# Reordering an S5 layer's parameter work beside the q, k and v projections of the layer before it

## The chip, the cores and the metric

One core of one Trainium2 chip runs the whole program. The time is device microseconds of one execution; lower is better.

## What is computed

A trunk of two layers over 512 tokens of width 1024, all in fp32. Layer 0 is block-sparse attention with rotary positions beside a multi-scale pooling branch; layer 1 is an S5 state-space branch beside a convolution. The parts that matter here, cut from the reference:

```python
def rope_partial(x):                       # the first 32 of 128 columns of a head
    x1 = xf[..., : ROT_DIM // 2]
    x2 = xf[..., ROT_DIM // 2: ROT_DIM]
    out = jnp.concatenate([x1 * cos - x2 * sin, x2 * cos + x1 * sin, xf[..., ROT_DIM:]], axis=-1)

def even_mixer(h, w_in, pool_w, pool_scale, w_out):
    z = h @ w_in
    q, k, v, ga, pu, gb = jnp.split(z, [A, 2 * A, 3 * A, 4 * A, 4 * A + POOL_WIDTH], axis=-1)
    q = rope_partial(q.reshape(b, s, ATT_HEADS, HEAD_DIM))
    k = rope_partial(k.reshape(b, s, ATT_HEADS, HEAD_DIM))

def s5_ssm(u, lam_re, lam_im, log_dt, b_re, b_im, c_re, c_im, d):
    dt = jnp.exp(log_dt.astype(f32))[:, None]
    mag = jnp.exp(lr * dt)
    ab_re = mag * jnp.cos(li * dt)
    ab_im = mag * jnp.sin(li * dt)
    den = lr * lr + li * li
    num_re = ab_re - 1.0
    f_re = (num_re * lr + ab_im * li) / den
    f_im = (ab_im * lr - num_re * li) / den
    bb_re = f_re[..., None] * br - f_im[..., None] * bi
    bb_im = f_re[..., None] * bi + f_im[..., None] * br
```

The S5 part that comes before any token is seen, `dt` to `bb`, depends on parameters alone. The kernel works it out while layer 0's projections run.

## The kernel before

**Projections.** Every fp32 product is three matmuls on split operands (`mm3`, L104 to L106: high by high, high by low, low by high), 128x512 each. The columns of the input projection are taken in groups: q, k, v (512 columns each), then `pg0`, `pg1`, `ga`. A group has four weight blocks of 512 KB (`raw`, three buffers); ACT rounds each to its high part (`whi`, L169), the DVE makes the low part (`wlo`, L61, two operations of 128x512 a block). `wblock` and `prefetch` run these ahead; SP issues all loads. The output of a group for four tiles of 128 tokens fills four PSUM banks `z`, and there are only four: the next group's tile t starts when this group's tile t has been read out.

**Reading out q and k.** `rope_evac` reads a bank: ACT copies the 96 columns that are not rotated (L602), the DVE rotates the other 32 in four operations:

```python
tt(V, q[:, :, 0:32], zv[:, :, 0:32], cosb, MUL)
tt(V, r[:, :, 0:16], zv[:, :, 16:32], sinb[:, :, 0:16], MUL)
tt(V, r[:, :, 16:32], zv[:, :, 0:16], sinb[:, :, 16:32], MUL)
tt(V, q[:, :, 0:32], q[:, :, 0:32], r, ADD)
```

The first three read the bank, the fourth reads SBUF only. In the trace they are `wt<-z,cs`, `r<-z,cs` (twice) and `wt<-wt,r`. TensorE transposes the rotated tiles (`tp`), and ACT (L109) and DVE (`qk<-tp,qk`) split them.

**S5 parameters.** `s5_loads` loads lambda (`lamn`), `ldt`, the state-major `b` (`b1`, `b2`, rows of 64 bytes), `cn` and `dm`. `s5_small` turns lambda with TensorE (L449, to `lam`) and `cn` (L456), masks `dm` on POOL, and works out exponential, sine and cosine in some hundred DVE operations of 128x32 (`mag`, `sn`, `cnn`, `fr`, `fi`, the powers `AR`, `AI`); then `b1` and `b2` are multiplied: `e<-b,fi`, `b<-b,fr` and their difference on the DVE, `pin<-b,fi`, `b<-b,fr` and their sum on POOL. `b<-b,fr` on the DVE writes over what POOL's `pin` reads. `s5_set_e(c)`, for four sets c, makes `e1` from `AR`, `AI`, `b1`, `b2` in three DVE operations of 128x512, and `g1` in three on POOL, and stores `g1`; `s5_set_p(c)` multiplies `e1` by a matrix `IC` on TensorE (four matmuls of 160 columns, L574) and stores the result. The last `set_p` adds `dm` to `kk` and stores lag kernels with eight DMAs (`kd`, L586). `s5_phasors` makes nine phasors `U` by repeated squaring on POOL, from `sn` and `cnn`: thirteen small operations a round, seven in the first. POOL then fills phasor tables `tab`, the first of which waits for the release of the pool of buffers that all this uses.

**What sets the order.** The list `after[group, block]` says behind which weight block a piece is emitted; `tc.issue_after(instruction)` keeps what is emitted in it behind that instruction. Within these a scheduler orders every engine's instructions by its own simulation; each engine then runs its own order strictly, each instruction waiting for its operands.

## Time and profile before

| | |
|---|---|
| median of 3 runs | 469.53 us (469.25 to 469.56) |
| profiled execution | 469.62 us, span of the trace 467.8 us |
| TensorE (PE) | busy 441.3 us, 94% of the span |
| VectorE (DVE) | 353.4 us, 76% |
| ScalarE (ACT) | 242.9 us, 52% |
| GpSimd (POOL) | 264.4 us, 57% |
| mean granted TensorE clock | 0.991 of full speed |

The profiled execution's own time and the span differ by 1.8 us that lie around the span. q's matmuls run up to 36 us, k's from 38 to 62, v's from 68 to 99.5. A timeline row gives the start, the duration, the engine, the line, the operation with output <- inputs, and in brackets how long the engine stood idle before and which instruction released it. Buffer numbers are left out of names. POOL's spans are rough.

### The profile page before, as it was taken

What the parts mean: (1) busy time and instruction counts of PE and PEld (TensorE: products, weight loads), DVE (VectorE), ACT (ScalarE), POOL (GpSimd) and SP (SyncE); (2) the same over time, 40 slices, a digit from 0 to 9 for tenths busy, and PEclk for the clock granted to TensorE, in tenths of its full rate; (3) what the DMA queues carried; (4) which work ended last, traced back from release to release, by engine and by line L of the source; (5) the groups of instructions that cost most, each with busy time, mean ns of one, the idle gap of its engine ahead of it and who ended that gap; (6) DMA issues with size and microseconds to landing.
All of it is one profiled execution on the core that took longest, in us unless ns stands there. A gap on an engine that the chain in (4) does not pass through costs nothing.

```text
span 467.8 us, 6759 instructions
## 1 busy us (share of the span) xinstructions
PE 441.3 (94%) x2185; PEld 361.9 (77%) x2185; DVE 353.4 (76%) x691; ACT 242.9 (52%) x437; POOL 264.4 (57%) x447
## 2 busy tenths in 40 slices
PE   6998959999988999979999999999999999999994
PEld 5886848888866888858879988777878777778884
DVE  2849999587698696773886397997999898666444
ACT  6644422555734744623685435657966336373421
POOL 1010798999999915480092385676999944421000
PEclk9999989999999999989999999999999999999999
DMA  7874233432422347441044794786434542132013
GB/s 266 191 179 143 91 113 135 120 89 76 135 73 83 118 135 252 158 138 41 3 122 132 179 246 137 208 214 176 125 93 121 153 141 75 71 91 89 1 61 120
DMA packets 62435, 59.58 MB, mean 127 GB/s; under 512 B 20569, under 2 KB 43745, under 8 KB 62400
## 3 DMA queue, kind: packets, MB, share of 16 engines
q1 hardware_dynamic: 62400, 59.16, 42.6%
q8 instruction: 17, 0.28, 0.2%
q14 instruction: 18, 0.15, 0.1%
HBM read 50.62 MB, written 8.52 MB: 126 GB/s over the span
## 4 chain that ended last, share of the span: by engine, by line
PE 59%; DVE 15%; POOL 13%; DMA 4%; ACT 4%; issue 3%; SPq 1%; DVEq 0%; ACTq 0%; POOLq 0%
PE z L104 17%; PE z L105 17%; PE z L106 17%; POOL tab L58 6%; DMA raw<-e_w_in 4%; POOL U L58 3%; DVE wlo L61 3%; POOL pa L58 2%; DVE wt L58 2%; PE s L979 2%; PE y L1014 1%; DVE wt L61 1%; PE y L1011 1%; DVE xh L61 1%; ACT junk L297 1%
## 5 line engine op out<-in xcount | busy, mean ns | idle before, releaser
L58 POOL TENSOR_TENSOR wlo<-raw,whi 128x1024 fp32r<-128x1024 f32 (+2 forms) x50 | 88.4, 1789 | 72.8 <-ACT whi L109 72.4
L104 PE MATMUL z<-hh,whi 128*128 128x512 f32 (+1 forms) x288 | 105.6, 374 | 2.0 <-DVE u L58 2.0
L105 PE MATMUL z<-hl,whi 128*128 128x512 f32 (+1 forms) x288 | 106.3, 370 | 0.0
L106 PE MATMUL z<-hh,wlo 128*128 128x512 f32 (+1 forms) x288 | 105.7, 369 | 0.0
L61 DVE SCALAR_TENSOR_TENSOR acc<-gp,dw,acc 128x512 f32<-128x512 f32 x100 | 75.1, 751 | 2.2
L109 ACT ACTIVATE whi<-raw 128x1024 fp32r<-128x1024 f32 (+2 forms) x54 | 45.3, 873 | 35.6 <-PE z L105 17.7
L104 PEld LDWEIGHTS z<-hh,whi 128*128 128x128 f32 x288 | 54.0, 189 | 12.0 <-DVE u L58 2.4
L106 PEld LDWEIGHTS z<-hh,wlo 128*128 128x128 f32 x288 | 54.4, 189 | 8.6 <-issue 0.2
L105 PEld LDWEIGHTS z<-hl,whi 128*128 128x128 f32 x288 | 54.4, 189 | 8.4 <-issue 0.3
L104 PE MATMUL z<-whi,hh 128*128 128x512 f32 x96 | 39.5, 415 | 9.6 <-DVE r L58 5.5
L61 DVE SCALAR_TENSOR_TENSOR wlo<-raw,gcol,whi 128x512 fp32r<-128x512 f32 x48 | 39.2, 839 | 9.6 <-ACT whi L169 9.5
L169 ACT ACTIVATE whi<-raw,gcol 128x512 fp32r<-128x512 f32 x48 | 32.1, 715 | 22.1 <-PE z L106 10.0
L105 PE MATMUL z<-wlo,hh 128*128 128x512 f32 x96 | 39.3, 412 | 0.0
L106 PE MATMUL z<-whi,hl 128*128 128x512 f32 x96 | 38.8, 404 | 0.0
L58 POOL TENSOR_TENSOR tab<-tab,U 128x4 f32<-128x4 f32 (+6 forms) x112 | 36.6, 358 | 0.0
L104 PEld LDWEIGHTS z<-whi,hh 128*128 128x128 f32 x96 | 18.7, 196 | 14.1 <-issue 5.9
L297 ACT ACTIVATE junk<-z 128x512 bf16<-128x512 f32 (+1 forms) x17 | 9.7, 570 | 30.7 <-PE z L106 30.7
L58 POOL TENSOR_TENSOR tab<-tab 128x4 f32<-128x4 f32 (+6 forms) x56 | 21.8, 409 | 0.0
L105 PEld LDWEIGHTS z<-wlo,hh 128*128 128x128 f32 x96 | 18.9, 196 | 3.6
L106 PEld LDWEIGHTS z<-whi,hl 128*128 128x128 f32 x96 | 18.6, 194 | 3.5
L58 POOL TENSOR_TENSOR pacc<-pacc,lt 128x512 f32<-128x512 f32 x14 | 18.9, 1351 | 0.2
L58 DVE TENSOR_TENSOR hl<-tp,hh 128x512 fp32r<-128x512 f32 x16 | 10.7, 682 | 9.5 <-ACT hh L109 9.5
(325 smaller groups left out, 1015.3 us busy)
## 6 DMA issues: line engine op xcount, KB each, us to landing
raw<-e_w_in SPq DMA_DIRECT2D x15, 512.0 KB, 4.7
raw<-e_w_in SPq DMA_DIRECT2D x18, 256.0 KB, 2.9
raw<-e_w_out SPq DMA_DIRECT2D x8, 512.0 KB, 3.8
raw<-o_w_in SPq DMA_DIRECT2D x16, 256.0 KB, 2.8
rot<-td SPq DMA_DIRECT2D x16, 256.0 KB, 6.0
raw<-o_w_in SPq DMA_DIRECT2D x8, 512.0 KB, 4.3
raw<-o_w_out SPq DMA_DIRECT2D x8, 512.0 KB, 3.7
qk<-x SPq DMA_DIRECT2D x8, 256.0 KB, 5.6
```

The costliest lines, as they stand in the source:

```text
L58: return e.tensor_tensor(o, a, b, op=op)
L61: e.scalar_tensor_tensor(o, a, s, b, op0=op0, op1=op1)
L104: nc.tensor.matmul(p, sh, mh, start=start, stop=False)
L105: nc.tensor.matmul(p, sh, ml, start=False, stop=False)
L106: return nc.tensor.matmul(p, sl, mh, start=False, stop=stop)
L109: i = S.activation(hi, src, AF.Copy)
L169: S.activation(hi[:, h], b.raw[:, h], AF.Copy, scale=gc)
L297: S.activation(jk[:, 0:src.shape[-1]], src, AF.Square, scale=1.0 / 32.0, accum_out=ss)
L979: nc.tensor.matmul(s[:, i], sets[m][0][hf, i], Ut[m][hf, i], start=True, stop=True)
L1011: nc.tensor.matmul(y[:, r], tb[:, m * 4 + r], Ut[m][:, r], start=True, stop=False)
L1014: nc.tensor.matmul(y[i * 64:i * 64 + 64, r], gt[:, g], xf[i][:, r], start=False, stop=True)
```

## The change

The order of loads: lambda and `ldt` are loaded by three DMAs instead of five, ahead of x's last tile, and lambda is turned by TensorE inside q, behind block 1 of tiles 0 and 1. The state-major `b` is issued behind the load of k's block 1, `cn` and `dm` behind the load of k's block 2.

The sets: E of sets 2 and 3 (DVE) is kept behind k's last rotation, G of sets 2 and 3 (POOL) behind the first four phasors, which are emitted behind k's block 2; the other five phasors stay where all nine were. The four `set_p` move from k1, k2, k3, v0 to k1, v0, v1, v2.

The rotation: both sine products first, then the cosine product in place in the bank, then the sum read from the bank.

```diff
+    lamn = pe.tile([32, 2, 2, 64], F32, name="lamn")
+    for i, nm in ((0, "o_lam_re"), (1, "o_lam_im")):
+        nc.sync.dma_start(lamn[:, i], A[nm][0].unsqueeze(1).to_broadcast([32, 2, 64]))
+    ldt = pe.tile([128, NG], F32, name="ldt")
+    nc.sync.dma_start(ldt, A["o_log_dt"][0:1, :].broadcast_to([128, NG]))
     load_x(xs0[3], 3)
...
+    def s5_lam():
         p = pt.tile([128, 2, NG], F32, tag="t", name="tp")
         for i in range(2):
-            nc.tensor.transpose(p[:, i], par["lamn"][:, i].rearrange("p a b -> p (a b)"), ident[0:32, 0:32])
+            nc.tensor.transpose(p[:, i], lamn[:, i].rearrange("p a b -> p (a b)"), ident[0:32, 0:32])
         S.activation(lam, p, AF.Copy)
...
-    def s5_phasors():
+    def s5_phasors(ks):
-        for k in range(9):
+        for k in ks:
...
-            tt(G, us, us, a1, MUL)
+            last_u[0] = tt(G, us, us, a1, MUL).ins
...
+        with tc.issue_after(last_rope[0]) if c > 1 else nullcontext():
+            for o, tab, w in ((e1, par["AR"][:, 1:], par["b1"]), (e2, par["AI"][:, 1:], par["b2"])):
...
+            tt(V, e1, e1, e2, ADD)
...
+        with tc.issue_after(last_u[0]) if c > 1 else nullcontext():
+            for o, tab, w in ((g1, par["GR"], par["ct1"]), (g2, par["GI"], par["ct2"])):
...
+            last_g[0] = tt(G, g1, g1, g2, ADD)
...
-    after["q", 0] += [s5_loads]
+    def late_loads():
+
+        with tc.issue_after(ld_ins[0].ins):
+            s5_loads()
+        load(index["k", 2] + 1)
+        with tc.issue_after(ld_ins[0].ins):
+            s5_loads2()
+    after["q", 0] += [late_loads]
     after["q", 0] += [s5_small]
...
-    for c, key in enumerate((("k", 1), ("k", 2), ("k", 3), ("v", 0))):
+    after["k", 2] += [lambda: s5_phasors(range(4))]
+    for c, key in enumerate((("k", 1), ("v", 0), ("v", 1), ("v", 2))):
...
-        tt(V, q[:, :, 0:32], zv[:, :, 0:32], cosb, MUL)
         tt(V, r[:, :, 0:16], zv[:, :, 16:32], sinb[:, :, 0:16], MUL)
         tt(V, r[:, :, 16:32], zv[:, :, 0:16], sinb[:, :, 16:32], MUL)
-        tt(V, q[:, :, 0:32], q[:, :, 0:32], r, ADD)
+        tt(V, zv[:, :, 0:32], zv[:, :, 0:32], cosb, MUL)
+        last_rope[0] = tt(V, q[:, :, 0:32], zv[:, :, 0:32], r, ADD).ins
...
         with tc.issue_after(last_g[0].ins):
-            s5_phasors()
+            s5_phasors(range(4, 9))
```

`ld_ins[0]` is the last weight load issued; `s5_loads2` holds the loads of `cn` and `dm` that stood in `s5_loads`.

What this does to the order on three engines, with buffer numbers. First TensorE from the end of k into v, before: `z_585` to `z_588` are k's banks for tiles 0 to 3, `z_898` to `z_901` v's, `tp_725` and `tp_730` belong to `set_p(0)`.

```order
L106 MATMUL z_588<-whi_613,hl1_129 128x512
L104 MATMUL z_588<-whi_613,hh1_127 128x512
L105 MATMUL z_588<-wlo_614,hh1_127 128x512
L106 MATMUL z_588<-whi_613,hl1_129 128x512
L104 MATMUL z_898<-whi_672,hh0_126 128x512
L105 MATMUL z_898<-wlo_673,hh0_126 128x512
L106 MATMUL z_898<-whi_672,hl0_128 128x512
...
L104 MATMUL z_899<-whi_672,hh0_126 128x512
L105 MATMUL z_899<-wlo_673,hh0_126 128x512
...
L574 MATMUL tp_725<-IC_349,e1_660 128x160 x2
L574 MATMUL tp_730<-IC_349,e1_660 128x160 x2
```

The same place with the change, where v's banks are `z_894` to `z_897`, `tp_728` and `tp_723` belong to `set_p(0)` and `tp_951` to `set_p(1)`:

```order
L105 MATMUL z_587<-wlo_612,hh1_138 128x512
L582 MATMUL tp_728<-IC_349,e1_658 128x160 x2
L106 MATMUL z_587<-whi_611,hl1_140 128x512
L104 MATMUL z_588<-whi_611,hh1_138 128x512
...
L106 MATMUL z_588<-whi_611,hl1_140 128x512
L104 MATMUL z_894<-whi_670,hh0_137 128x512
L639 MATMUL tp_716<-ident_81,rsy_310 128x128 x4
L105 MATMUL z_894<-wlo_671,hh0_137 128x512
...
L582 MATMUL tp_951<-IC_349,e1_736 128x160 x2
L104 MATMUL z_894<-whi_748,hh0_137 128x512
L105 MATMUL z_894<-wlo_749,hh0_137 128x512
L104 MATMUL z_895<-whi_670,hh0_137 128x512
```

`set_p(0)` began behind v's first 24 matmuls; now its first half stands in k, seven matmuls before v, and a piece of `set_p(1)` before v's ninth matmul, the first on `z_895`. `z_895` needs the bank of `z_586`.

Next the DVE from the products with `b` to the rotation of k, before, where `e1_660` and `e1_738` are E of sets 0 and 1:

```order
L58 TENSOR_TENSOR e2_483<-b2_321,fi_452 128x512
L58 TENSOR_TENSOR qk_556<-tp_704,qk_555 128x4x128
L58 TENSOR_TENSOR qk_556<-tp_711,qk_555 128x4x128
L58 TENSOR_TENSOR b1_320<-b1_320,fr_451 128x512
L58 TENSOR_TENSOR b1_320<-b1_320,e2_483 128x512
L61 SCALAR_TENSOR_TENSOR wlo_809<-raw_678,gcol_97,whi_808 128x512 x2
L58 TENSOR_TENSOR e1_660<-AR_440,b1_320 128x512
L58 TENSOR_TENSOR e1_738<-AR_440,b1_320 128x512
L58 TENSOR_TENSOR wt_869<-z_585,cs_115 128x4x32
L58 TENSOR_TENSOR r_870<-z_585,cs_115 128x4x16 x2
```

With the change, where `e1_658` and `e1_736` are E of sets 0 and 1, and `r_866` and `r_873` belong to the rotations of tiles 0 and 1:

```order
L58 TENSOR_TENSOR b1_323<-b1_323,fr_451 128x512
L58 TENSOR_TENSOR b1_323<-b1_323,e2_483 128x512
L58 TENSOR_TENSOR r_866<-z_585,cs_126 128x4x16
L58 TENSOR_TENSOR e1_658<-AR_440,b1_323 128x512
L58 TENSOR_TENSOR e1_736<-AR_440,b1_323 128x512
...
L58 TENSOR_TENSOR wt_865<-z_585,r_866 128x4x32
L58 TENSOR_TENSOR e2_659<-AI_441,b2_324 128x512
L61 SCALAR_TENSOR_TENSOR wlo_671<-raw_609,gcol_103,whi_670 128x512 x2
L58 TENSOR_TENSOR e1_658<-e1_658,e2_659 128x512
...
L61 SCALAR_TENSOR_TENSOR wlo_831<-raw_676,gcol_103,whi_830 128x512 x2
L58 TENSOR_TENSOR r_873<-z_586,cs_126 128x4x16 x2
L58 TENSOR_TENSOR z_586<-z_586,cs_126 128x4x32
```

The rotation of tile 1 stood directly behind that of tile 0; now the rest of E of sets 0 and 1, six weight splits and two `qk` stand between them.

Last POOL from `dm` to `pin`, before, with `U` the phasors:

```order
L58 TENSOR_TENSOR dm_329<-dm_329,ident_81 32x16x16 x2
L552 COPY IC_349<-ct1_337 128x4x32 x2
L528 COPY U_134<-sn_355 64x16 x2
L528 COPY U_134<-cnn_356 64x16 x2
...
L521 COPY GI_492<-AI_441 128x32 x2
L58 TENSOR_TENSOR g1_665<-GR_491,ct1_337 128x512
L58 TENSOR_TENSOR g1_743<-GR_491,ct1_337 128x512
L58 TENSOR_TENSOR g2_666<-GI_492,ct2_338 128x512
L58 TENSOR_TENSOR pin_484<-b1_320,fi_452 128x512
...
L58 TENSOR_TENSOR g1_860<-g1_860,g2_861 128x512
L58 TENSOR_TENSOR pa1_1479<-U_134 128x16
```

With the change:

```order
L58 TENSOR_TENSOR dm_334<-dm_334,ident_81 32x16x16 x2
L534 COPY U_145<-sn_355 64x16 x2
L58 TENSOR_TENSOR pa2_781<-U_145 128x16
...
L558 COPY IC_349<-ct1_337 128x4x32 x2
L58 TENSOR_TENSOR pa1_788<-U_145 128x16
...
L58 TENSOR_TENSOR pa1_802<-U_145 128x16
L58 TENSOR_TENSOR pa2_803<-U_145 128x16
...
L58 TENSOR_TENSOR g1_663<-GR_491,ct1_337 128x512
L58 TENSOR_TENSOR g1_741<-GR_491,ct1_337 128x512
L58 TENSOR_TENSOR U_145<-U_145 128x16
...
L58 TENSOR_TENSOR pin_484<-b1_323,fi_452 128x512
L58 TENSOR_TENSOR g2_664<-GI_492,ct2_338 128x512
```

The phasors stood behind all twelve operations of G. Now the rounds 0, 1 and 2 and the start of round 3 stand ahead of `pin`, and G of sets 2 and 3 behind round 3.

## Rows read from the trace of the kernel before

**Rows 1.** TensorE's waits over the whole span: us in total, times, longest.
```profile
PE z L104 <- DVE r L58: 5.5, 1, 5.5
PE z L106 <- DVE qk L58: 3.2, 1, 3.2
PE z L104 <- DVE tmp L61: 2.1, 1, 2.1
```

**Rows 2.** Timeline of PE: start us, us, engine, line, operation, [idle <-releaser].
```profile
28.72 0.60 PE L456 MATMUL tp<-ident,e 128*128 128x128 f32 x4
...
67.86 0.77 PE L104 MATMUL z<-whi,hh 128*128 128x512 f32 x1 [5.51 <-DVE r L58]
...
71.11 0.39 PE L106 MATMUL z<-whi,hl 128*128 128x512 f32 x1
...
74.74 1.25 PE L574 MATMUL tp<-IC,e 128*128 128x160 f32 x8
75.72 0.50 PE L104 MATMUL z<-whi,hh 128*128 128x512 f32 x1
```

**Rows 3.** Windows: PE, PEld, DVE, ACT, POOL busy; PEclk, DMA share, GB/s.
```profile
37.00:38.00 1.00, 0.00 (x0) 0.01 (x1) 1.00 (x8) 1.00 (x4) 0.00 (x0) 1.00 0.21 80
...
40.00:62.00 22.00, 22.00 (x109) 18.26 (x107) 20.85 (x75) 8.44 (x14) 12.86 (x20) 1.00 0.28 89
...
68.00:70.00 2.00, 2.00 (x5) 1.61 (x6) 2.00 (x5) 0.00 (x0) 1.92 (x3) 0.50 0.33 120
...
204.00:207.00 3.00, 3.00 (x8) 2.35 (x8) 3.00 (x2) 0.99 (x2) 3.00 (x2) 0.50 0.66 187
```

**Rows 4.** Timeline of DVE from 55 to 70.
```profile
55.52 1.27 DVE L58 TENSOR_TENSOR qk<-tp,qk 128x512 fp32r<-128x512 f32 x2
57.63 1.54 DVE L58 TENSOR_TENSOR b<-b,fr 128x512 f32<-128x512 f32 x1 [0.84 <-POOL pin L58]
...
64.00 3.25 DVE L58 TENSOR_TENSOR e<-AR,b 128x512 f32<-128x512 f32 x2
67.18 0.28 DVE L58 TENSOR_TENSOR wt<-z,cs 128x128 f32<-128x128 f32 x1
...
68.82 1.23 DVE L58 TENSOR_TENSOR wt<-wt,r 128x128 f32<-128x128 f32 x1
```

**Rows 5.** Timeline of DVE at 77, where POOL does no large operation.
```profile
77.09 0.68 DVE L58 TENSOR_TENSOR e<-AI,b 128x512 f32<-128x512 f32 x1
```

**Rows 6.** Timeline of POOL from 28 to 58.
```profile
28.77 1.54 POOL L58 TENSOR_TENSOR dm<-dm,ident 32x256 f32<-32x256 f32 x2 [26.29 <-DMA dm<-o_d]
...
45.51 0.46 POOL L528 COPY U<-sn 64x16 f32<-64x16 f32 x2 [11.32 <-DVE sn L58]
...
56.55 1.05 POOL L58 TENSOR_TENSOR pin<-b,fi 128x512 f32<-128x512 f32 x1
```

**Rows 7.** Timeline of SP's queue, where the loads are issued, from 26 to 31.
```profile
26.33 0.96 SPq L442 DMA_DIRECT2D dm<-o_d  x2
27.39 0.39 SPq L146 DMA_DIRECT2D raw<-e_w_in  x1
27.82 0.47 SPq L760 DMA_DIRECT2D pscale<-e_pool_scale  x1
...
30.45 0.61 SPq L822 DMA_DIRECT2D gb<-o_glu_b  x1
```

**Rows 8.** Timeline of POOL in the first three phasor rounds.
```profile
73.87 0.83 POOL L58 TENSOR_TENSOR pa<-U 128x16 f32<-128x16 f32 x2
...
82.95 0.39 POOL L58 TENSOR_TENSOR pa<-U 128x16 f32<-128x16 f32 x2
...
85.44 0.39 POOL L58 TENSOR_TENSOR pa<-U 128x16 f32<-128x16 f32 x2
```

**Rows 9.** Timeline of DVE, attention's mask added to scores in PSUM.
```profile
99.64 0.29 DVE L58 TENSOR_TENSOR s<-s,mask 128x128 f32<-128x128 f32 x1
```

**Rows 10.** Timeline of POOL where the phasor tables begin.
```profile
100.58 0.11 POOL L726 MEMSET tab<- 128x4 f32 x1
```

More of the change, by code (lines that the diff above doesn't have):

```diff
@@ L115, in tile_hybrid_trunk @@
         pass
-    order, index, blocks, loaded, emitted = [], {}, {}, [0], [0]
+    order, index, blocks, loaded, emitted, ld_ins = [], {}, {}, [0], [0], [None]
     def wp_block():
@@ L236, in tile_hybrid_trunk @@
     qp = l0.enter_context(tc.tile_pool(name="qp", bufs=5))
+    l0p = {"pk": l0.enter_context(tc.tile_pool(name="pk", bufs=1))}
+    pstk = ExitStack()
+    pe = pstk.enter_context(tc.tile_pool(name="pe", bufs=1))
     def big():
@@ L347, in tile_hybrid_trunk @@
     Kd = dr.tile([NI, NG // 2, 2, Q, NI], F32, tag="kd", name="kd", bufs=1)
-    l0p = {nm: l0.enter_context(tc.tile_pool(name=nm, bufs=1)) for nm in ("pk",)}
-    pstk = ExitStack()
-    pe = pstk.enter_context(tc.tile_pool(name="pe", bufs=1))
     par = {}
@@ L425, in s5_loads @@
     def s5_loads():
-        lamn = pe.tile([32, 2, 2, 64], F32, name="lamn")
-        for i, nm in ((0, "o_lam_re"), (1, "o_lam_im")):
-            for d in range(2):
-                nc.sync.dma_start(lamn[:, i, d], A[nm][0])
-        ldt = psm("ldt")
-        nc.sync.dma_start(ldt, A["o_log_dt"][0:1, :].broadcast_to([128, NG]))
         b1 = pe.tile([128, NG, NI], F32, name="b1")
@@ L442, in s5_loads, with s5_small @@
             nc.sync.dma_start(dm[r].rearrange("p g c -> p (g c)"), A["o_d"][0:1, :].broadcast_to([32, 512]))
-        par.update(lamn=lamn, ldt=ldt, b1=b1, b2=b2, cn=cn, dm=dm)
-    def s5_small():
-        lam = pe.tile([128, 2, NG], F32, name="lam")
+        par.update(cn=cn, dm=dm)
+    lam = pe.tile([128, 2, NG], F32, name="lam")
+    def s5_lam():
         p = pt.tile([128, 2, NG], F32, tag="t", name="tp")
         for i in range(2):
-            nc.tensor.transpose(p[:, i], par["lamn"][:, i].rearrange("p a b -> p (a b)"), ident[0:32, 0:32])
+            nc.tensor.transpose(p[:, i], lamn[:, i].rearrange("p a b -> p (a b)"), ident[0:32, 0:32])
         S.activation(lam, p, AF.Copy)
+    def s5_small():
         lr, li = lam[:, 0], lam[:, 1]
@@ L467, in s5_small @@
         dt, mag, th, sn, cn_ = psm("dt"), psm("mag"), psm("th"), psm("sn"), psm("cnn")
[L468 removed]
+        pexp(dt, ldt)
         tt(V, mag, lr, dt, MUL)
```

27 lines of the change are left out of this document (13 added, 14 removed).

## The prediction

> **What bounds it now.** I read three views in turn: TensorE's waits, its timeline around the longest ones, and the DVE's timeline over the same stretch. TensorE's waits [rows 1] name DVE work in three of the largest places; two lie where this change works. 2.1 us go before k's first matmul, which starts at 38.02, and 5.5 before v's first at 67.86 [rows 1, 2]. v's first matmul needs the bank that tile 0 of k left, and that bank is free when its rotation has read it. TensorE is not merely late by the wait: after these 5.5 us the granted clock is 0.50 of full speed, the 1.2 GHz level, from 68 to 70, while at k's start it stays 1.00 [rows 3]. The ninth matmul of v, which starts at 71.11 [rows 2], is my mark: before it seven matmuls ran at about 0.43 us instead of 0.23, about 1.4 us in all.
>
> Why is the rotation late? The DVE's row from 55.5 to 67.2 has no real gap but 0.84 us: six operations of 128x512 that read two SBUF operands stand ahead of the rotation and take about 1.6 us each, 9.55 us for the six from 57.63 to 67.18 [rows 4]. With POOL at other work the same kind takes 0.68 [rows 5]. So each pays for a POOL operation beside it; `qk<-tp,qk`, which reads PSUM, pays nothing at the same time (1.27 us for two) [rows 4]. The chain behind it is the S5 parameters: `b<-b,fr` on the DVE overwrites what POOL's `pin` reads, and `pin` ends at 57.6 [rows 6]. I call the end of `pin` P. Before, P is 57.6.
>
> **The change, part by part.** The edits in set placement, load order and phasors act on one number, P, and on what the DVE must do between P and the rotation.
>
> *k's start.* q now finishes two token tiles early, so their rotation runs inside q and the 2.1 us go. In their place stands a possible wait: the four transposes of `cn` are 13 matmuls from q's end, and `cn` is loaded later. TensorE comes there at about 31.9. Today they start at 28.72 without a wait [rows 2], so `cn` has landed by then; 3.3 us later (the shift below) is 32.0, and a weight load between may make it 33.5. That is 0.1 to 1.6 us; I take 0.8. k would start at 36.7 instead of 38.02, and TensorE would reach the first set's transposes (`tp_728`), still in k, 22.2 us later, at 58.9. By the sum below they can't start there, so these 1.3 us are not in the sum: they make a later wait longer.
>
> *When POOL can begin.* In POOL's program `dm` comes first, and everything of this stage stands behind its two operations of 1.54 us together, which now start at 28.77 [rows 6]. SP issues `dm` at 26.33 [rows 7], so it lands within 2.4 us. In the new order five small loads, the first at 27.82 and the last at 30.45, 0.5 us of issue each, and the weights of k1 and k2, 0.39 each, pass ahead of it [rows 7]: 2.5 + 0.8 = 3.3 later, landing at 32.0. The weights of k1 and k2, 0.5 MB each, now pass through the DMA engines just before, which may add one or two; I take 33, so POOL is free at 34.5. The lambda is there long before, and by the DVE's new order I estimate that its sine and cosine end about then.
>
> *P.* Before, POOL waits until 45.51 for the sine, then goes from copies straight to the sets [rows 6]. Now three phasor rounds stand ahead of `pin`. A quiet round takes 2.5 us (82.95 to 85.44), the first, without squaring, about 1.5; two rounds beside a full DVE took 9.1 us (73.87 to 82.95) where quiet ones would take 4 [rows 8]. Quiet: 34.5 + 0.9 (four copies at 0.23 [rows 6]) + 6.5 + 2.0 for eight smaller copies + 2.1 for two set products at `pin`'s 1.05 + 0.6 + 1.05 = 47.7. With the loud rounds five more, 52.7. In this stretch the DVE has eight weight splits and many operations of 128x32, which hold POOL briefly; I take 1.2 more than quiet, **P = 48.9**, between 47 and 53. The DVE waits for it at `b<-b,fr` from about 46 on (34.5, eight splits at 0.66, some 25 small operations at 0.11, `qk` and rotations 3.5), and four banks of k wait in its queue behind that instruction.
>
> *From P to the ninth matmul.* By the new order it needs the rotation of `z_586`. Before this the DVE has 14 operations of 128x512 with two SBUF operands, two of `qk` and two rotations. Bounds: all beside POOL, 14x1.59 = 22.3; none, 14x0.68 = 9.5; and 2.7 for the rest. POOL has nine 128x512 operations in its own row there, the others are phasor pieces of 0.2 us. 9x1.59 + 5x0.68 = 17.7, + 2.7 = 20.4; I add 1.3 for the small pieces and for the wait of `e2_659` for POOL's `b2`: 21.7. So 48.9 + 21.7 = 70.6 against 71.1: **-0.5 us**.
>
> *Rotation in PSUM.* The addition that cost 1.23 us [rows 4] now reads PSUM, and takes what `wt<-z,cs` does, 0.28; that is already in the 2.7. The product written back to PSUM has no row of its own kind in k, but attention's mask addition works in place there, in 0.29 us a 128x128 [rows 9]. The bank is held one operation longer, 0.2 us, inside the 2.7 too.
>
> *What is left behind the mark.* Six parameter matmuls that came later now stand ahead of the mark, in its shade: 6x0.12 = **-0.7 us**, since eight take 0.98 us today, from 74.74 to the next matmul at 75.72 [rows 2].
>
> *The clock.* The loss of 1.4 us lies before the mark of 71.1 and is part of it. The new standstill comes in pieces, about 3.1 us before `tp_728`, then 2 to 3, 1 to 1.5 and 1.7. A wait of 3.2 us at 200 to 203 brought 0.50 for 204 to 207 [rows 3]; 2.08 brought nothing. So the price lies between 0 and 1.4 us behind the mark, and not below 0, since the clock is 1.00 there today. I take 0: the last pieces are as short as the harmless one.
>
> *Later.* The last set goes from k's end to v's end, so the lag kernels' eight DMAs, today well before POOL's tables start at 100.58 [rows 10], come about 7 us later. POOL then fills tables without 4.9 us of phasors between them, so they end about 2.7 us later. On ACT `pwh` waits in both orders for the same release, with a softmax piece and its transposes behind it; by the order TensorE comes to these some 14 us after v's end, and they are released 9 to 12 after it: nothing, with an upper bound of 2 us. The phasors moved ahead fill POOL's idle 30 to 45 and are worth nothing by themselves.
>
> Sum: -0.5 - 0.7 = -1.2. The profiled execution took 469.62, so 468.42; the median of the runs is 0.09 lower, which gives **468.3**. About 0.2%, 0.94 us, is what a measurement here can tell from no change.
>
> **The rivals.**
> - *The chain is early enough* (0.20). If dm lands by 31 and POOL's rounds are quiet, P is 45 to 46; if POOL's small pieces also let the DVE run at 0.68 for half of the 14, the mark is reached after 16 us. The limit is TensorE itself: from 58.9 on 7 matmuls of k, 8 of v and some transposes, 63.5 unstalled. Gain 7.6 + 0.7 at most, 461.2; with half of it 465.4. For it: POOL idles from 30 to 45 today. Against it: `dm` ahead of everything on POOL.
> - *POOL pays for the phasors* (0.28, slower). Ahead of `pin` three rounds run beside a DVE that is 95% busy from 40 to 62 [rows 3]. If they take as the loud row does, P is 52.7 and each microsecond of P is one of time: +3.8 on the forecast, 472.1. It decides from P = 51: 0.94 + 1.2 = 2.1 above my 48.9.
> - *The clock stays low through the pieces* (0.08, no change). The 1.2 GHz level after a standstill lasted two to three microseconds both times [rows 3]; with four pieces inside twelve microseconds it may cover the matmuls behind the mark as well: +1.4, 469.7. The Trainium skill (TensorE: Matmul & The Clock Gate, What's actually happening) says that the level follows how busy TensorE has lately been; by that rule pieces with few matmuls between them are as bad as one long wait, and the two rows with 0.50 agree that standing still lowers it, and none of before shows waits in pieces.
> - *The end of v waits for the lag kernels* (0.12). Slack of about 2 us is thin; +0.5 to +3 on the forecast, 468.8 to 471.3, half of it no change.
>
> **How the numbers follow.** The forecast has 0.32: its own range is 466.4 to 469.9 (P 47 to 50.5), and gives faster 0.22, same 0.10. With the chain early (0.20, all faster), the phasors' price (0.28, all slower), the clock (0.08: same 0.05, faster 0.02, slower 0.01) and the lag kernels (0.12: slower 0.07, same 0.04, faster 0.01): faster 0.45, same 0.19, slower 0.36. The range reaches from a good half of the early chain's gain, 462.5, to P = 53 with a little of the lag kernels' price, 473.5.
>
> **What would show it.** Right: no gap at 36 to 38; POOL's `pin` ending near 49; TensorE stopped before `tp_728`, about 3 us, and again before `z_895`; additions `wt<-z,r` of 0.28. Wrong: `pin` after 51 (then slower), or no stop of TensorE between 58 and 71 (then 462). If pg0 opens early but `s` or `tp` there waits for ACT, the lag kernels were the price.

## The result, and the profile after

The median of 20 runs is 475.12 us, against 469.25 (20 runs) for the kernel before on the same chip: 5.9 us slower, and above the range of 462.5 to 473.5 that was forecast. The runs of the change lie between 467.48 and 484.78, those of before between 468.61 and 472.16. The ratio, 1.0064 [1.004, 1.0089], leaves out runs more than 1.5% above a kernel's fastest, which for the change, with one run at 467.48, are eleven of twenty. By the ratio the change is slower by 0.4 to 0.9% and takes 1.0064 x 469.25 = 472.3, inside the range; by either figure it is slower. This scatter is part of the finding. The profiled execution of the change took 473.96 (span 472.2), against 469.62.

TensorE's waits (us in total, times, longest), to set beside [rows 1]:
```profile
PE tp L713 <- DVE P L65: 6.0, 3, 3.4
PE tp L582 <- POOL pa L67: 3.5, 1, 3.5
PE z L106 <- DVE qk L58: 3.2, 1, 3.2
...
PE tp L713 <- DVE nm L65: 1.6, 1, 1.6
...
PE tp L462 <- DMA e<-o_c_im: 0.9, 1, 0.9
```
The 2.1 us before k and the 5.5 before v are gone. In their place stands one wait of 3.5 in k, and a line that the kernel before does not have: `tp`, attention's transposes of P, waits for the DVE's normalisation of P, 6.0 us. The 1.6 us put down to `nm` belong with it: that `nm` stands directly behind a slow P on the DVE.

TensorE's timeline, the places of [rows 2] and the one where the time goes:
```profile
32.41 0.63 PE L462 MATMUL tp<-ident,e 128*128 128x128 f32 x4 [0.86 <-DMA e<-o_c_im]
...
61.75 0.81 PE L582 MATMUL tp<-IC,e 128*128 128x160 f32 x4 [3.48 <-POOL pa L67]
...
69.47 0.47 PE L104 MATMUL z<-whi,hh 128*128 128x512 f32 x1 [0.38 <-DVE wt L58]
...
162.55 0.27 PE L106 MATMUL o<-ph,vl 128*128 128x128 f32 x1
166.20 0.48 PE L713 MATMUL tp<-ident,P 128*128 128x128 f32 x1 [3.38 <-DVE P L65]
168.01 0.90 PE L713 MATMUL tp<-ident,P 128*128 128x128 f32 x3 [1.33 <-DVE P L65]
168.56 0.78 PE L104 MATMUL z<-hh,whi 128*128 128x512 f32 x1
169.14 0.63 PE L105 MATMUL z<-hl,whi 128*128 128x512 f32 x1
```
The windows, with the columns of [rows 3]:
```profile
62.00:66.00 4.00, 4.00 (x15) 3.15 (x15) 4.00 (x7) 1.38 (x4) 4.00 (x4) 0.57 0.72 259
66.00:70.00 4.00, 3.62 (x21) 2.92 (x20) 3.93 (x12) 2.81 (x8) 3.92 (x4) 1.00 0.38 121
...
168.00:171.00 3.00, 2.99 (x9) 2.52 (x10) 3.00 (x5) 1.03 (x3) 0.10 (x1) 0.50 0.21 24
```
To see where the time goes, count the matmuls that write a projection bank `z` and compare the start of the n-th in both traces (each trace has 1,704 of them; the first 288 are those of q, k and v):

| n | before | change | difference | what lies before it |
|---|---|---|---|---|
| 216 | 74.52 | 72.98 | -1.5 | v's first blocks |
| 288 | 98.58 | 95.43 | -3.1 | end of v |
| 360 | 118.64 | 115.36 | -3.3 | attention, first rows |
| 384 | 127.45 | 129.05 | +1.6 | a stop of about 4.9 us |
| 432 | 147.87 | 144.32 | -3.6 | before has its own stops here |
| 480 | 160.98 | 157.50 | -3.5 | |
| 504 | 170.90 | 173.96 | +3.1 | a stop of 6.5 us |
| 648 | 213.23 | 217.50 | +4.3 | the last 1.2 us |

So the change does what its first half was meant to do. It is 3.1 us ahead at the last matmul of v (n = 288), and still 3.5 ahead at n = 480. Then 6.5 us go in one place, far behind everything that it touches. There TensorE stands 3.38 us, does one transpose, stands another 1.33, and starts again at the lower level: the starts of eight matmuls from 168.56 to 171.66 are 3.10 us apart where seven steps of 0.23 are 1.6, so 1.5 more. Together 6.2 of the 6.5.

(The expectations below call v's last matmul the 289th. Some of their figures are those of a matmul beside it: 98.26 for the kernel before, which is 98.58 here, 95.87 for e7, which is 96.09, and 94.19 for e16, which is 93.96.)

What TensorE waits for stands in the DVE's timeline:
```profile
50.04 1.58 DVE L58 TENSOR_TENSOR b<-b,fr 128x512 f32<-128x512 f32 x1 [6.25 <-POOL pin L58]
...
69.05 0.28 DVE L58 TENSOR_TENSOR wt<-z,r 128x128 f32<-128x128 f32 x1
...
113.58 7.16 DVE L65 TENSOR_SCALAR P<-P,rs 128x384 f32<-128x384 f32 x1
...
158.84 0.16 DVE L705 RECIPROCAL rs<-su 128x1 f32<-128x1 f32 x1 [2.90 <-ACT P L704]
159.04 7.11 DVE L65 TENSOR_SCALAR P<-P,rs 128x384 f32<-128x384 f32 x1
166.07 0.68 DVE L58 TENSOR_TENSOR u<-z,rbc 128x512 f32<-128x512 f32 x1
```
A softmax row is divided by its sum in one instruction, `ts(V, P[:, :nk], P[:, :nk], rs, None, MUL)`. The other instances of that form in layer 0 take 0.28 to 0.83 us; these two take 7.16 and 7.11, and nothing they wait for is shown. Beside them POOL runs the last steps of a phasor table:
```profile
32.62 2.02 POOL L58 TENSOR_TENSOR dm<-dm,ident 32x256 f32<-32x256 f32 x2 [30.14 <-DMA dm<-o_d]
...
48.94 1.07 POOL L58 TENSOR_TENSOR pin<-b,fi 128x512 f32<-128x512 f32 x1
...
106.19 0.11 POOL L744 MEMSET tab<- 128x4 f32 x1 [15.32 <-DMA kd<-kk]
...
158.38 1.07 POOL L58 TENSOR_TENSOR tab<-tab,U 128x64 f32<-128x64 f32 x4
159.38 0.63 POOL L58 TENSOR_TENSOR tab<-tab 128x64 f32<-128x64 f32 x2
159.94 1.50 POOL L58 TENSOR_TENSOR tab<-tab,U 128x128 f32<-128x128 f32 x4
161.38 0.91 POOL L58 TENSOR_TENSOR tab<-tab 128x128 f32<-128x128 f32 x2
162.21 2.35 POOL L58 TENSOR_TENSOR tab<-tab,U 128x256 f32<-128x256 f32 x4
164.49 1.43 POOL L58 TENSOR_TENSOR tab<-tab 128x256 f32<-128x256 f32 x2
```
A table is built by doubling: steps of six operations, 4 columns wide, then 8, and so on to 256, all reading and writing SBUF, back to back. The second P starts inside the 64-column step and ends 0.23 us after the 256-column step does, at 166.15 against 165.92. POOL is not slowed: four operations of 256 columns take 2.35 us here, and 2.93 at 132.66, where the DVE gets through. Here one engine is shut out, and the other goes at its own pace.

The trace of before has one such operation too. It was there to be read, and the prediction did not use it:
```profile
127.35 5.42 DVE L65 TENSOR_SCALAR P<-P,rs 128x128 f32<-128x128 f32 x1
```
TensorE then waits 2.0 us. Two operations and 7.6 us of waits in one trace (1.58 and 1.27 behind the first, 3.38 and 1.33 behind the second), one operation and 2.0 in the other: the question for the experiments is what shuts the DVE out, and why the change gets more of it.

### The profile page after: what moved, and what is told of

It reads as the page before. It is cut to its first block, busy times and chain, and to the rows that moved or that the text cites. A ratio compares the mean times of both kernels' runs of the same rounds, so it can differ in the third digit from the quotient of the medians.

```text
span 472.2 us, 6758 instructions
## 1 busy us (share of the span) xinstructions
PE 445.0 (94%) x2185; PEld 366.1 (78%) x2185; DVE 354.6 (75%) x691; ACT 242.0 (51%) x437; POOL 264.9 (56%) x447
## 4 chain that ended last, share of the span: by engine, by line
PE 68%; DVE 17%; POOL 5%; ACT 3%; DMA 3%; issue 3%; SPq 1%; DVEq 0%; ACTq 0%; POOLq 0%
PE z L104 20%; PE z L105 19%; PE z L106 19%; DVE P L65 3%; DVE wlo L61 2%; PE s L997 2%; DVE wt L58 2%; PE y L1032 1%; PE y L1029 1%; DVE wt L61 1%; DMA qk<-x 1%; DVE xh L61 1%; POOL U L58 1%; DMA ldt<-o_log_dt 1%; DVE qk L58 1%
## 5 line engine op out<-in xcount | busy, mean ns | idle before, releaser
L106 PE MATMUL z<-hh,wlo 128*128 128x512 f32 (+1 forms) x288 | 106.9, 374 | 0.0
L104 PE MATMUL z<-hh,whi 128*128 128x512 f32 (+1 forms) x288 | 106.9, 377 | 0.0
L104 PE MATMUL z<-whi,hh 128*128 128x512 f32 x96 | 38.5, 411 | 2.2 <-ACT whi L169 1.8
L58 POOL TENSOR_TENSOR tab<-tab,U 128x4 f32<-128x4 f32 (+6 forms) x112 | 35.2, 349 | 0.0
L58 POOL TENSOR_TENSOR tab<-tab 128x4 f32<-128x4 f32 (+6 forms) x56 | 22.8, 429 | 0.0
L65 DVE TENSOR_SCALAR P<-P,rs 128x128 f32<-128x128 f32 (+3 forms) x16 | 20.5, 1284 | 0.3
```

The lines of the kernel that those rows point to most:

```text
L58: return e.tensor_tensor(o, a, b, op=op)
L65: e.tensor_scalar(o, a, s1, None, op0=op0)
L104: nc.tensor.matmul(p, sh, mh, start=start, stop=False)
L106: return nc.tensor.matmul(p, sl, mh, start=False, stop=stop)
```

## The experiments

The first theory, A, is the form: the division is a tensor_scalar, and that form needs something POOL holds. Its rival, B, is the stretch: any DVE operation that comes at a bad moment of POOL's table is shut out until the table ends, and which one comes there is decided by when each engine arrives. A further question runs beside both: which part of the change earns the 3.1 us at v's end. Every run was compared with the kernel before on the same chip (its medians in the five groups of runs: 469.77, 469.68, 470.06, 469.18 and 469.87). Medians and ranges are of all runs; the ratios are formed as above.

| run | median us (lowest to highest) | ratio to before |
|---|---|---|
| e1_after_tt | 473.73 (468.77 to 476.78) | 1.0044 [1.0008, 1.008] |
| e2_before_tt | 471.72 (470.16 to 496.32) | 1.0046 [1.0025, 1.0066] |
| e3_after_short_tables | 462.72 (460.79 to 466.27) | 0.9859 [0.9819, 0.9898] |
| e4_before_tt_rot | 474.22 (473.22 to 2459.02) | 1.0086 [1.006, 1.0113] |
| e5_after_gaps | 472.54 (470.21 to 874.53) | 1.0042 [1.0024, 1.0061] |
| e6_before_short_tables | 465.39 (463.90 to 468.23) | 0.9904 [0.9874, 0.9933] |
| e7_after_old_sets | 465.55 (462.82 to 469.89) | 0.9918 [0.9881, 0.9955] |
| e8_after_old_rotation | 465.78, one run | none |
| e9_after_act_scale | 471.08 (467.84 to 480.78) | 1.0025 [0.9998, 1.0053] |
| e10_before_act_scale | 473.91 (472.19 to 475.49) | 1.0088 [1.0059, 1.0116] |
| e11_after_old_sets_act | 471.26 (468.50 to 472.16) | 1.0018 [0.9995, 1.0041] |
| e12_after_shift | 475.17 (470.84 to 476.72) | 1.0101 [1.0064, 1.0138] |
| e13_after_gaps_again | 473.03, one run | none |
| e14_after_wide_step_dve | 466.44 (465.99 to 467.41) | 0.9945 [0.993, 0.9961] |
| e15_old_sets_wide_step_dve | 467.86 (464.33 to 469.18) | 0.9957 [0.9934, 0.9981] |
| e16_old_sets_old_rotation | 470.57 (467.31 to 497.35) | 1.0003 [0.9979, 1.0027] |
| e17_loads_wide_step_dve | 467.95 (465.87 to 469.82) | 0.9964 [0.9942, 0.9986] |
| e18_loads_breaks | 469.97 (468.12 to 471.29) | 0.9998 [0.9973, 1.0024] |

### Is it the form? e1, e2, e9, e10

e1 (on the change) and e2 (on the kernel before) divide with another instruction:
```
-            ts(V, P[:, :nk], P[:, :nk], rs, None, MUL)
+            tt(V, P[:, :nk], P[:, :nk], rs.to_broadcast([128, nk]), MUL)
```


> The changed kernel with one edit: the softmax scaling P*rs on the DVE is a tensor_tensor with rs broadcast instead of a tensor_scalar. Theory A (the tensor_scalar form is locked out for as long as POOL issues table operations back to back, 7.16 and 7.11 us in the changed kernel; the form matters): no P over 2.5 us, the gain of 3.3 us that stood at the start of pg1 is kept to the end, 465 to 467 us, and the runs lie within 1.5 us instead of 17. Theory B (every DVE operation on SBUF is held by these POOL stretches, and the loss comes from the tables being later): P still has entries over 5 us, 472 to 476, spread as before. Theory C (the loss is the clock after short waits, not P): P may get short, but 471 or more remains.

> The kernel before with the same one edit. Theory A: the one P of 5.42 us at 127.35 goes to 1.5 or less and TensorE's wait of 2.0 us behind it goes, 466.5 to 469.2, never over 470 (today one run of 20 is at 472). Theory B: no change, 469.3, with a P over 4 us.

e1 gave 1.0044, e2 1.0046, and P is shut out as before. In e1's profile, the DVE:
```profile
163.54 5.48 DVE L58 TENSOR_TENSOR P<-P,rs 128x384 f32<-128x384 f32 x1
```
It starts in a 128-column step at 163.54 and ends at 169.02, 0.42 us after POOL stops. POOL stops one operation before the end of the 256-column step, because it has to wait for the DVE:
```profile
167.86 0.74 POOL L58 TENSOR_TENSOR tab<-tab 128x256 f32<-128x256 f32 x1
173.14 0.10 POOL L799 MEMSET ub<- 128x2 f32 x1 [4.54 <-DVE wt L61]
173.20 2.85 POOL L58 TENSOR_TENSOR tab<-tab 128x256 f32<-128x256 f32 x1
```
In e2 there are two, 3.36 us and 6.24 where the kernel before had one. The form theory falls.

e9 (the change) and e10 (before) take the division away from the DVE altogether:
```
-            ts(V, P[:, :nk], P[:, :nk], rs, None, MUL)
+            S.activation(P[:, :nk], P[:, :nk], AF.Copy, scale=rs)
```


> The changed kernel with the softmax scaling P*rs on ACT instead of the DVE; POOL's tables stay whole. Theory A2 (an operation of the DVE with its operands in SBUF is sometimes shut out until a dense stretch of POOL's tables ends, and the time is lost where TensorE waits for that operation): no operation of the DVE over 2 us from 100 to 165 in front of which TensorE waits, 463 to 467, spread under 4 us. If other operations of the DVE fall into the trap in P's place, or ACT becomes the wait: 469 to 474.

> The control: the kernel before with the scaling on ACT. Theory A2: its one shut-out P (5.42 us) goes, 467 to 469; so the change is worth 2.5 to 4 us once the tables can't take it back. If the difference between this and the changed kernel with the same edit is under 1 us, the gain at v is lost in another way than through P.

e9 gave 1.0025, e10 1.0088. In both, others stand in P's place. The DVE of e9:
```profile
118.79 4.25 DVE L61 SCALAR_TENSOR_TENSOR wlo<-raw,gcol,whi 128x512 fp32r<-128x512 f32 x1 [0.45 <-ACT whi L169]
...
160.71 5.54 DVE L58 TENSOR_TENSOR ub<-u 128x527 f32<-128x527 f32 x1
```
and the longest of all, on the DVE of e10:
```profile
153.89 8.00 DVE L61 SCALAR_TENSOR_TENSOR wlo<-raw,gcol,whi 128x512 fp32r<-128x512 f32 x1
```
with POOL beside it:
```profile
153.72 1.06 POOL L58 TENSOR_TENSOR tab<-tab,U 128x64 f32<-128x64 f32 x4
...
160.50 0.12 POOL L775 MEMSET u<- 128x16 f32 x1
160.54 0.11 POOL L781 MEMSET ub<- 128x1 f32 x1
160.60 0.74 POOL L58 TENSOR_TENSOR tab<-tab 128x256 f32<-128x256 f32 x1
```
The same weight split takes about 0.7 elsewhere. It ends at 161.89, 0.55 after the table's last operation (161.34); the two memsets between did not let it in. So a tensor_scalar, a tensor_tensor and a scalar_tensor_tensor, of 16 to 527 columns, are all shut out. B holds, if the table's end is read as the end of POOL's stretch, as e1 shows. e10 missed the 467 to 469 expected of it: with the division on ACT the kernel before becomes slower.

### Is it the table's wide steps? e3 and its control e6

The steps of 64 columns and more are left out, and two memsets put in their place, in the change (e3) and in the kernel before (e6):
```
-                cmul(G, c[:, :, n:2 * n], s[:, :, n:2 * n], c[:, :, 0:n], s[:, :, 0:n], br, bi, x1, x2)
+                if k < 4:
+                    cmul(G, c[:, :, n:2 * n], s[:, :, n:2 * n], c[:, :, 0:n], s[:, :, 0:n], br, bi, x1, x2)
+                else:
+                    G.memset(c[:, :, n:2 * n], 0.0)
+                    G.memset(s[:, :, n:2 * n], 0.0)
```


> The changed kernel with the three widest doubling steps of the phasor tables replaced by memsets, so part of the tables is not computed; P stays a tensor_scalar. Theory A: with no long stretch of wide table operations on POOL no P is over 2 us, 464 to 467, spread under 2 us. Theory C or a cost that has nothing to do with POOL's tables: 471 or more.

> The kernel before with the three widest doubling steps of the tables as memsets, so part of the tables is not computed: the control for the changed kernel with the same cut, which took 462.7. If the change's gain at v (2.8 to 3.3 us) is real and the tables alone take it back, this is 465.5 to 468, about 3.5 us above that run. If the cut itself makes the gain (less work on POOL), it is within 1 us of 462.7.

e3 gave 0.9859, and its 462.72 is below the 464 to 467 expected; the two longest divisions, back to back, take 1.48 us together, and TensorE's waits have no line on P. This rules out theory C of the expectations, a cost of the clock without P, for which 471 or more was expected. e6 gave 0.9904. So by the ratios the wide steps cost the change 1.0064 - 0.9859 = 2.05%, or 9.6 us, and the kernel before 0.96%, or 4.5; by the medians of all runs it is 12.4 and 4.3. Without the wide steps the change is worth 465.39 - 462.72 = 2.7 us by the medians and 2.1 by the ratios, somewhat less than the 3.1 that it has at the end of v. The 5.1 us between the two prices (8.1 by the medians) are what turned a gain into a loss. The control is what makes this a statement on the change: e3 alone would have shown only that leaving work out is faster.

### Which part earns, which part loses? e7, e8, e16, e4

e7 puts the sets back to k's end and the phasors back into one piece:
```
-        with tc.issue_after(last_rope[0]) if c > 1 else nullcontext():
+        with nullcontext():
...
-    after["k", 2] += [lambda: s5_phasors(range(4))]
-    for c, key in enumerate((("k", 1), ("v", 0), ("v", 1), ("v", 2))):
+    for c, key in enumerate((("k", 1), ("k", 2), ("k", 3), ("v", 0))):
...
-            s5_phasors(range(4, 9))
+            s5_phasors(range(9))
```


> The changed kernel with the sets, their order and all nine phasors as in the kernel before; the early lambda, the late loads and the rotation in PSUM stay. I read the 289th matmul on a bank z, near v's end: 98.26 in the profile before, 95.43 with the change. If the split of the sets and phasors carries the gain: 97.5 or later. If the early lambda carries it (POOL's pin then ends 4 us or more before 50.0, since no phasor stands ahead of it): 96 or earlier. POOL's tables start near 100 and not at 106 in both cases; the whole time hangs on the P's that fall into them, 465 to 474.

It gave 0.9918, faster than both kernels. At v's end it is 2.5 us ahead of before, against the change's 3.1: a hair behind the mark of 96 that was set for the loads, and far from the 97.5 for the sets. `pin` ends at 46.6, 3.5 us before the change's and not 4. But POOL's tables begin twelve microseconds earlier, since POOL does not stand 15.3 us waiting for `kd`:
```profile
94.39 0.10 POOL L743 MEMSET tab<- 128x4 f32 x1
...
153.17 1.43 POOL L58 TENSOR_TENSOR tab<-tab 128x256 f32<-128x256 f32 x2
```
and in its profile no DVE operation takes over 1.9 us from 100 to 165. Its runs still scatter over 7 us.

e8 puts the old rotation back, with the sum in SBUF:
```
+        tt(V, q[:, :, 0:32], zv[:, :, 0:32], cosb, MUL)
...
-        tt(V, zv[:, :, 0:32], zv[:, :, 0:32], cosb, MUL)
-        last_rope[0] = tt(V, q[:, :, 0:32], zv[:, :, 0:32], r, ADD).ins
+        last_rope[0] = tt(V, q[:, :, 0:32], q[:, :, 0:32], r, ADD).ins
```


> The changed kernel with the rotation as before (the product with cos to SBUF first, the sum of two SBUF operands). If the rotation in PSUM carries 1 us or more of the gain at the 289th matmul on z (95.43 with the change), it comes at 96.4 or later, and the additions take 1.0 us or more each beside POOL. If it is worth nothing there, 95.0 to 96.

One run, 465.78; at v's end it is 4.2 us ahead, so more than the change and past the 95.0 to 96 expected. e16 has the edits of e7 and the old rotation, which leaves of the change only the early lambda and the late loads (below: the loads alone):

> Of the change the early lambda and the late loads alone; sets, phasors and rotation as before. With the rotation undone but the sets kept the 289th matmul on a bank z came at 94.43, with the sets undone but the rotation kept at 95.87, with both parts at 95.43. If the loads carry the gain alone: 94.5 to 96. If the rotation in PSUM is needed when the sets are as before: 97 or later. Time 462 to 470, by the tables' shut-outs.

It gave 1.0003, but is 4.6 us ahead at v's end. Of all profiles with the new loads, the four with the old rotation stand at -3.5 to -4.6 there and the ten others that can be read at -1.2 to -3.4. So the loads carry the gain at v, and neither the split of the sets nor the rotation in PSUM adds to it. How much the rotation in PSUM costs is open: kernels that differ from the change only behind v already lie between -1.2 and -3.3. What e16 has won it loses in another way, by TensorE's waits:
```profile
PE tp L712 <- DVE P L65: 8.3, 1, 8.3
```
The division named is short (e17's expectation takes it for a P of 8 us, which it is not). The DVE stands ahead of it:
```profile
136.88 1.36 DVE L58 TENSOR_TENSOR wt<-ub,rcnt 128x16 f32<-128x16 f32 x1 [8.78 <-POOL ub L58]
138.17 0.66 DVE L61 SCALAR_TENSOR_TENSOR wt<-ub,u 128x496 f32<-128x496 f32 x1
138.75 0.34 DVE L65 TENSOR_SCALAR P<-P,rs 128x256 f32<-128x256 f32 x1
```
and on POOL the addition of the pooling layer that it waits for has its turn only inside the table:
```profile
133.51 2.31 POOL L58 TENSOR_TENSOR tab<-tab,U 128x256 f32<-128x256 f32 x4
135.79 1.06 POOL L58 TENSOR_TENSOR ub<-u 128x527 f32<-128x527 f32 x1
```
This is a second way for a table to stop TensorE, in which no operation of the DVE is drawn out: an operation that someone waits for stands behind others in POOL's own queue.

e4 adds the rotation in PSUM, with e2's division, to the kernel before.

> The kernel before with the tensor_tensor form of P and, of the change, the rotation in PSUM alone. If the sets and the phasors carry the gain at the start of v, this is within 1 us of the run without the rotation (TensorE's wait before v 4.5 to 5.5 us, since two additions at 1.2 us stand behind the first rotation, not ahead of it). If the rotation carries it, the wait before v falls below 3.5 us and the time is 2 us or more below.

474.22 us, ratio 1.0086 [1.006, 1.0113], 2.5 above e2. Its profiled execution took 2,459 us, so the wait before v could not be read: inconclusive on the mark, and no sign of a gain.

### Does the moment decide? e12

Fourteen memsets on POOL, about 4 us, behind the first table move all others later:
```
+                with (tc.issue_after(shift[0]) if shift else nullcontext()):
+                    cmul(G, c[:, :, n:2 * n], s[:, :, n:2 * n], c[:, :, 0:n], s[:, :, 0:n], br, bi, x1, x2)
+            if h == 0:
+                last = tt(G, gapt[:, 0:4], s[:, 0, 124:128], c[:, 0, 124:128], ADD).ins
+                for _ in range(14):
+                    with tc.issue_after(last):
+                        last = G.memset(gapt, 0.0).ins
+                shift.append(last)
```


> The changed kernel with 14 memsets of 128x256 on POOL, about 4 us, between the first of the four tables and the others. Nothing is left out; POOL has more work and its tables end 4 us later. Theory A2: which P falls into a dense stretch is a matter of where they stand in time, so more work on POOL can make the kernel faster: the P of 128x384 near 159, in front of which TensorE waited, is met at another place; 465 to 472, and the P's over 4 us are others than those at 113.6 and 159.0. If it is the lateness of the tables that costs, this is 477 or more.

It gave 1.0101. In its profile the two divisions that took 7 us take 0.41 (at 113.76) and 2.08 (155.35), and the matmul of n = 480 starts 6.5 us ahead of before. Then it is lost: another operation, `ub` at 167.03, waits 3.52 for POOL and is itself shut out 6.05 us, and TensorE waits 7.3. So the moment decides which operation falls in; moving POOL by some microseconds is no remedy, it draws another lot.

### Breaks in the tables: e5, e13, e18

Behind each operation of the wide steps stands a memset of one column, kept there by `issue_after`:
```
...
+                for args in ((x1, ai, bi, MUL), (x2, ar, bi, MUL), (co, ar, br, MUL), (co, co, x1, SUB), (so, ai, br, MUL), (so, so, x2, ADD)):
+                    with (tc.issue_after(last_gap[0]) if last_gap[0] is not None else nullcontext()):
+                        i = tt(G, *args)
+                    with tc.issue_after(i.ins):
+                        last_gap[0] = G.memset(gapt, 0.0).ins
```


> The changed kernel with a memset of one column on POOL behind each of the six operations of the three widest doubling steps of the tables, as a break in POOL's dense stretches; nothing is left out. Theory A2 (any DVE operation with operands in SBUF may be shut out as long as POOL reads SBUF back to back without a break, the operation's form does not matter): the breaks let it in, no P over 2 us, 464 to 467 us and a spread under 3 us. Theory D (what matters is how much POOL reads, not whether there are breaks): P entries over 4 us as before, 470 to 476.

> The kernel with breaks in POOL's table stretches once more, for an undisturbed profile. If a break of one memset lets a waiting DVE operation in (theory A2), no operation of the DVE between 100 and 165 lasts over 2 us, and what remains above 466 is a wait that the longer tables make; if breaks don't let it in, there are entries of 4 us or more that span several memsets.

e5 gave 1.0042 [1.0024, 1.0061], but its profiled execution took 620 us and can't be read; e13 is the same kernel run once more (473.03). There no DVE operation between 100 and 165 takes over 1.9 us. But the tables end at 177 instead of 166, and the DVE now waits for small operations in POOL's longer queue:
```profile
167.56 0.71 DVE L58 TENSOR_TENSOR ub<-ub 128x524 f32<-128x524 f32 x1 [4.05 <-POOL gapt L761]
...
175.62 0.71 DVE L58 TENSOR_TENSOR ub<-u 128x527 f32<-128x527 f32 x1 [2.59 <-POOL gapt L761]
```
It is 4.4 us ahead at n = 504 and 2.1 behind at 528. e18 takes the loads alone, with the breaks, and moves the pooling layer's memsets to the DVE, so that these waits should go:
```
-        G.memset(u[:, 0:16], 0.0)
+        V.memset(u[:, 0:16], 0.0)
...
-            G.memset(b[:, 0:step], 0.0)
+            V.memset(b[:, 0:step], 0.0)
```


> The early lambda and the late loads alone, the tables whole on POOL with a memset as a break behind each operation of the three widest steps, and the small memsets of the pooling branch on the DVE instead of POOL. The breaks left no DVE operation over 2 us between 100 and 165, and what was lost then were waits of the DVE of 4.05 and 2.59 us for memsets that stood behind the tables in POOL's queue; these go. 462.5 to 466. If the longer tables (about 13 us more) are waited for elsewhere: 468 or more.

0.9998: a miss. No DVE operation takes over 1.9 us in its tables either, and it is 6.6 us ahead at n = 408; then the DVE stands 10.25 us for POOL's `ub`, which is the second way again, by the additions that were left on POOL.

### A shorter stretch: e14, e15, e17, and e11

e14 is the change with the table's widest step, six operations of 256 columns, on the DVE:
```
-                cmul(G, c[:, :, n:2 * n], s[:, :, n:2 * n], c[:, :, 0:n], s[:, :, 0:n], br, bi, x1, x2)
+                cmul(V if k == 6 else G, c[:, :, n:2 * n], s[:, :, n:2 * n], c[:, :, 0:n], s[:, :, 0:n], br, bi, x1, x2)
```


> The changed kernel with the widest doubling step of each table (six operations of 256 columns) on the DVE instead of POOL; nothing left out. POOL's dense stretch ends after the step of 128 columns, about 4 us earlier than now. Theory A2: no wait of the DVE over 4.5 us, one shut-out costs at most half of today's; 464 to 470. If the length of the stretch is not what sets the loss: 472 to 476.

0.9945, faster than both kernels, and its four runs lie within 1.4 us. The stretch on POOL is 3.8 us shorter and the tables end at 159.2; in its profile no DVE operation is shut out while they run, and n = 504 starts 6.8 us ahead of before. The same step in e7 (e15) and in the loads alone (e17):

> The kernel with the early lambda, the late loads and the rotation in PSUM, with sets and phasors as before, and the widest step of the tables on the DVE. If the spread of that kernel (462.8 to 469.9) comes from shut-outs to the end of a stretch: 462 to 466, spread under 4 us. If the DVE's 9 us of added work count: 467 to 471.

> The early lambda and the late loads alone, with the widest step of the tables on the DVE. The loads alone put the 289th matmul on a bank z at 94.19, 4.1 us ahead of before, and lost it to one P of 8 us; the widest step on the DVE took the shut-outs from the changed kernel (466.4, within 1.4 us). Together: 463.5 to 466, spread under 3 us, ahead of both kernels. If the split sets and the rotation are needed for a steady time: 467 or more, or a spread over 4 us.

0.9957 and 0.9964: faster than before, but both missed what was hoped for, 462 to 466 and 463.5 to 466, and their twelve runs each spread over 4.9 and 4.0 us. The step is not free, since the DVE waits for POOL's narrower steps with its whole queue behind; the DVE of e17:
```profile
105.98 0.66 DVE L58 TENSOR_TENSOR tab<-tab,U 128x256 f32<-128x256 f32 x1 [7.59 <-POOL tab L58]
```
TensorE waits 4.4 us there. e11 is e7 with the division on ACT:

> The early lambda, the late loads and the rotation in PSUM, with sets and phasors as before, and the scaling on ACT: the version that should beat both. 462 to 464, runs within 3 us, if the spread of 462.8 to 469.9 of that kernel with the scaling on the DVE comes from P's shut out in some runs; 465 or more with the same spread if not.

1.0018, a miss: three weight splits are shut out, 4.49, 6.62 and 4.72 us. e7's gain is thus not safe either; its tables only happen to fall well.

Of the versions that beat both kernels, e7 has the lowest median (465.55, over 7 us of scatter in ten runs) and e14 the narrowest range (466.44), but on four runs only. Their intervals overlap, so which is faster stays open.

Over all profiles the two remedies look alike. Of the eleven with the tables whole on POOL and without breaks, nine have a DVE operation of over 2.5 us in the tables; of the seven with the wide steps cut, the widest step on the DVE, or breaks, none has. Breaks alone are two of the seven, and e7 and e8 have none without any remedy, so that the breaks let the DVE in is likely, not shown.

## Why the prediction was wrong, step by step

- **k's start** was right: the wait for `cn` is 0.86 us where 0.8 was taken, and k's own gap is gone.
- **When POOL can begin** was right: `dm` lands at 32.6 (33 was taken), and its two operations, 2.02 instead of 1.54 us, leave POOL free at 34.6 (34.5).
- **P** is 50.0 where 48.9 was forecast, within the bounds of 47 and 53. The DVE waits 6.25 us for it, as described. The rival in which POOL pays for the phasors did not come: P stayed below 51. But that each microsecond of P is one of time, as that rival has it, is not borne out: P is 46.6 in e7, 46.4 in e16 and 51.7 in e8, and v's end is 2.5, 4.6 and 4.2 us ahead of before. The phasors moved ahead of `pin` put it 3.5 us later without a visible price there.
- **From P to the ninth matmul** took 69.47 - 50.0 = 19.5 us, not 21.7: too many operations were priced as loud (the 14 operations take 15.1 us, where 17.7 was taken). The mark lies 1.6 us earlier than before, not 0.5. TensorE stopped before `tp_728` for 3.48 us (3.1 forecast), but before `z_895` for only 0.38.
- **Rotation in PSUM**: the addition takes 0.28, as forecast. That this saves anything on the path is not seen: kernels with the old rotation are further ahead at v's end.
- **What is left behind the mark**: v ends 3.1 us earlier, 1.5 more than the mark, where 0.7 was taken.
- **The clock**: the lower level lies at 62 to 66 (0.57), ahead of the mark, and 66 to 70 has 1.00. Nothing was lost behind it, as taken.
- **Later** is the step that failed: "nothing, with an upper bound of 2 us". It followed the lag kernels' DMAs and ACT, and weighed lateness. The DMAs are later (`kd` is issued from 98.51, before from 90.01), POOL waits 15.32 us for them, and the tables begin at 106.19 instead of 100.58 [rows 10]. They end only 1.4 us later (the prediction says 2.7, though its own 7 less 4.9 is 2.1), so lateness is not the cost. The cost is the new meeting of two engines: with TensorE and the DVE three microseconds earlier and POOL six later, other operations fall into the tables' wide steps, and two that TensorE waits for were shut out for 7 us. Between n = 480 and 504 that is 6.5 us, where the sum has 0.

So the sign was lost on a term that the sum did not contain. At v's end the change is better than forecast (3.1 us against 1.2), and from 288 to 648 it gives back 3.1 + 4.3 = 7.4. The 0.36 given to a slower kernel stood on other causes: the phasors' price on P, which did not come, and the lag kernels behind v, where at n = 360 the change is still 3.3 us ahead. That some chance lay on this side is luck, not insight. No row of the prediction showed the DVE beside a table, though before's own 5.42 at 127.35 was in the trace. e6 puts the price that before pays for its wide steps at 4.5 us: a change that moves one engine against the other there can gain that much or lose as much again, and the range should have been widened by it on both sides.

What stays open: why some DVE operations pass between two table operations and others don't. In the change's profile a division of 128x128 that starts in a 128-column step at 148.10 takes 0.28, while the step goes on. Another, at 128.29, takes 0.83, and ends 0.08 after POOL stops in the step to wait for the DVE, so it is a short case of the same kind. And the 467.48 us of one run of the change, 7.6 below the median, is what a run would take that meets no shut-out operation; no profile of such a run was taken, so that is argued, not shown.

## What to carry to other kernels

Look in the trace of before not only at the mean of an instruction form but at its longest instance, and at what the neighbouring engine did meanwhile: one P of 5.42 us among fifteen of under one is a price that any shift in time can multiply or remove. Where a long stretch of one engine can stop another, shorten the stretch or take it off the path before tuning what lies ahead of it, since gains made earlier otherwise become lots drawn there; and undo the parts of a change one at a time, for here the loads alone carried the gain. Operations that others wait for do not belong in a queue behind long stretches, which cost as much here (8.3 us) as being shut out.
